# Four one-bank score accumulators in place of two two-bank tiles in branch B of an encoder layer

## The chip, the core and the metric

The kernel runs as one program on one core of a Trainium2 chip. The core has five engines with an instruction queue each: TensorE (PE in the profile, with its weight loads listed apart as PEld), VectorE (DVE), ScalarE (ACT), GpSimd (POOL) and SyncE (SP, which here only issues DMAs). Each engine takes its instructions in order; semaphores make one wait for another. Matmul results land in PSUM, eight banks of 512 float32 per partition. The metric is the device time of one execution in microseconds, lower is better. Before the change it is 2105.86 us, the median of three runs (2105.69 to 2107.47).

## The reference

One layer of an encoder with two token mixers runs over two sequences, `x_prompt` (1024 tokens) and `x_sample` (512 tokens), with a model width of 1024. The change sits in the second mixer, a neighbourhood attention on a grid 64 tokens wide:

```python
z = rmsnorm(x) @ w_in            # q_A k_A v_A q_B k_B v_B gate_A gate_B
o_a = grouped_query_attention(q_A, k_A, v_A)             # branch A
# branch B, 8 heads of 64, window of 8 rows x 16 columns:
s = einsum('bqhd,bkhd->bhqk', q_B, k_B) * scale + bias   # bias by 2-D offset
s = where(mask, s, -1e30)
o_b = softmax(s) @ v_B
mix = (sigmoid(gate_A) * (o_a @ w_proj_a) + sigmoid(gate_B) * (o_b @ w_proj_b)) @ w_out
x = x + mix
x = x + relu(rmsnorm(x) @ w_up)**2 @ w_down
y = rmsnorm(x)
```

## The kernel before

The two sequences are two trunks, s0 (512 tokens, names with `0_`) and s1 (1024 tokens, names with `1_`). Each goes through branch A, branch B (pool `phB0` or `phB1`) and a merge stage (`phG`); the MLP of both follows. Most matmuls are made of three (`mm3`, L266 to L268), from a high and a low part of each operand.

PSUM is shared out as two tiles of two banks (`pbig`, made by `big`, L90 and L108) and four tiles of one bank (`pmm`, made by `mm`). Branch A, the merge and others use both kinds.

Branch B works in units. A unit `u = (h, js)` is one head and, in s1, one of four column strips `j`, with two halves of the rows (`hf`); in s0 it is one head and a pair of strips, one half each. So a unit always has two score blocks, `x` = 0 and 1, called its halves below. `s_unit` computes them: for each half two matmuls into the scores (L1164, high and low part of the keys), one VectorE instruction that adds the bias and the mask and finds the row's extreme (L1166, which reads the scores in PSUM and writes `sbs`, with its accumulator into `msbs`), and the exponential on ScalarE (L1170). GpSimd makes the bias block (L1150). In s1 `planes` then normalises and splits the weights into two float16 planes (ScalarE L1191, VectorE L1192) and SP transposes them by DMA (L1195); in s0 `t_unit` transposes on PE (L1209). `v_unit` does the product with the values (L1237) and hands it on (L1244, L1245). Before the change both halves of a unit live in one `big` tile, each in its own bank:

```python
s = big(f"sb{N}_{h}_{js[0]}")
...
so = s[:, x * 512 : x * 512 + nkey]
for i in range(2):
    nc.tensor.matmul(so, q, kv[i], start=(i == 0), stop=(i == 1))
```

`nkey` is 384 in s1 and 256 in s0. Between the steps of a unit PE gets other work, pulled from a list (`fill`): the gate matmuls (`gps`), the projection of branch A (`ppas`, from L1040 on) and the projections of queries and keys (`pqb`, `pkb`).

The program's order is not written out by hand. The loop gives each engine its instructions, and the framework's scheduler then places them and works out the semaphores from the tiles and their buffers: a tile that takes over a buffer waits until the earlier one has been read. The order on each engine is fixed when the program is built.

Of the kernel before, what the change touches and what calls it, by code (L numbers as in the profile page):

```python
# [11 lines left out]
F32 = mybir.dt.float32  # L12
# [7 lines left out]
P = 128  # L20
# [54 lines left out]
def encoder(ctx: ExitStack, tc: tile.TileContext, xs, outs, w):  # L75
# [4 lines left out]
    mix = ctx.enter_context(ExitStack())  # L80
# [6 lines left out]
    rawp = mix.enter_context(tc.tile_pool(name="rawp", bufs=3))  # L87
    sgp = mix.enter_context(tc.tile_pool(name="sgp", bufs=2))
    s8l = mix.enter_context(tc.tile_pool(name="s8l", bufs=NLEFT))
    pbig = mix.enter_context(tc.tile_pool(name="pbig", bufs=2, space=bass.MemoryType.PSUM))  # L90
    pmm = mix.enter_context(tc.tile_pool(name="pmm", bufs=4, space=bass.MemoryType.PSUM))


    hd = dram.tile([NTOK, D], F32, name="hd")
# [2 lines left out]
    def phase(name, bufs=2):  # L97
        return tc.tile_pool(name=name, bufs=bufs, reuse_waits="tile")
# [8 lines left out]
        return pmm.tile([P, 512], F32, tag="mm", name=name)  # L107

    def big(name):
        return pbig.tile([P, 1024], F32, tag="big", name=name)  # L110


    ident = cst.tile([P, P], F32, name="ident")
# [28 lines left out]
    def first_norm(xt, gb, row, g8, ones, pool, nm):  # L142

        warm_up(6)
        pt = big("grow")
        for q in range(2):
            qs = slice(q * 512, q * 512 + 512)
            nc.tensor.matmul(pt[:, qs], ones, row[:, qs], start=True, stop=True)
        pg = mm("g8")[:, 0:NC8]
        tc.keep_in_program_order(nc.tensor.transpose(pg, g8, ident[0:NC8, 0:NC8]))  # L150
        gcol = sml.tile([P, 8], F32, tag="ms", name="gcol")
        xn = pool.tile([P, D], F32, tag="xn", name=f"xn{nm}", bufs=2)
        ss = sml.tile([P, 8], F32, tag="ss", name=f"ss{nm}")
        tc.keep_in_program_order(nc.scalar.activation(xn, xt, AF.Square, accum_out=ss[:, 0:1]))
        r = rstd(ss[:, 0:1], 1, D, nm, True)

        def spread():
            for q in range(2):
                qs = slice(q * 512, q * 512 + 512)
                tc.keep_in_program_order(nc.scalar.activation(gb[:, qs], pt[:, qs], AF.Copy))  # L160

        def rest():
            for q in range(2):
                qs = slice(q * 512, q * 512 + 512)
                tc.keep_in_program_order(
                    nc.vector.tensor_scalar(xn[:, qs], xt[:, qs], r[:, 0:1], None, op0=ALU.mult)
                )
            tc.keep_in_program_order(nc.vector.tensor_scalar(gcol, pg, 1.0, None, op0=ALU.mult))
            return xn, gcol

        return rest, spread, pt

    def warm_up(n):

        pt = big("warm")
        for i in range(n):
            nc.tensor.transpose(pt[:, i % 8 * P : (i % 8 + 1) * P], ident, ident)
# [172 lines left out]
    def transpose_tile(xn, dest, j, nm, pin=False, between=()):  # L350

        pt = big(f"pt{nm}")
        for c in range(NC8):
            nc.tensor.transpose(pt[:, c * P : (c + 1) * P], xn[:, c * P : (c + 1) * P], ident)
        view = [
            (
                pt[:, q * 512 : (q + 1) * 512].rearrange("p (c t) -> p c t", t=P),
                dest[0][q][:, :, j * P : (j + 1) * P],
                dest[1][q][:, :, j * P : (j + 1) * P],
            )  # L360
            for q in range(2)
        ]
        for src, hi, lo in view:
            op = nc.scalar.activation(hi, src, AF.Copy)
            if pin:
                tc.keep_in_program_order(op)
        for i, (src, hi, lo) in enumerate(view):
            for step in between[i : i + 1]:
                step()
            op = nc.vector.tensor_tensor(lo, src, hi.bitcast(F32), op=ALU.subtract)  # L370
            if pin:
                tc.keep_in_program_order(op)
# [120 lines left out]
    def run(tr, nxt, first):  # L493
        N, x, T, NT, NB = tr.N, tr.x, tr.T, tr.NT, tr.NB
# [83 lines left out]
        for g in range(2):  # L578
            with phase(f"phR{N}_{g}") as ph:
# [168 lines left out]
                for tt in range(NT):  # L748
                    tb, j = divmod(tt, 4)
                    nm = f"{N}_{g}_{tt}"  # L750
# [17 lines left out]
                    js = slice(j * P, (j + 1) * P)  # L768
# [115 lines left out]
            with phase(f"phA{N}_{g}") as ph:  # L884
# [79 lines left out]
                for ui, u in enumerate(units):  # L964
                    h, qb = u
# [88 lines left out]
        nkc = kr_n // 4  # L1054
        nkey = kr_n * 32
        nq = rows * 16
        with phase(f"phB{N}") as ph:
            JN = 3 - halves
            msk = ph.tile([P, halves * 3, nkey], BF16, tag="msk", name=f"msk{N}", bufs=1)
# [73 lines left out]

            def s_unit(u):
                h, js = u
                s = big(f"sb{N}_{h}_{js[0]}")
                p = ph.tile([P, 2, nkey], F32, tag="pb", name=f"pb{N}_{h}_{js[0]}", bufs=2)
                nm_, l, rl = (
                    sml.tile([P, 8], F32, tag=n_, name=f"{n_}b{N}_{h}_{js[0]}") for n_ in ("ms", "ss", "rs")
                )  # L1140
                for x, (j, hf) in enumerate((j, hf) for j in js for hf in range(halves)):
                    nm = f"{N}_{h}_{j}_{hf}"
                    ct = (0, 1, 1, 2)[j]
                    c0 = (0, 8, 24, 32)[j]
                    jr = (16, 8, 8, 0)[j]
                    r0 = 0 if hf == 0 else 4
                    ir = 4 if hf == 0 else 0
                    if j != 2:
                        bm = ph.tile([P, nkey], F32, tag="bm", name=f"bm{nm}", bufs=4)
                        nc.gpsimd.tensor_tensor(  # L1150
                            bm.rearrange("p (r c) -> p r c", c=32),
                            rects[h][:, ir : ir + kr_n, jr : jr + 32],
                            msk[:, hf * 3 + ct, :].rearrange("p (r c) -> p r c", c=32),
                            op=ALU.add,
                        )
                        bms[hf] = bm
                    bm = bms[hf]
                    q0 = j * (T // 4) + hf * P
                    so = s[:, x * 512 : x * 512 + nkey]
                    for i in range(2):  # L1160
                        kv = qk[h // 2][1][h % 2][:, i, :].rearrange("p (r c) -> p r c", c=GRID_W)[
                            :, r0 : r0 + kr_n, c0 : c0 + 32
                        ]
                        nc.tensor.matmul(so, qk[h // 2][0][:, h % 2, q0 : q0 + P], kv, start=(i == 0), stop=(i == 1))  # L1164
                    sb = ph.tile([P, nkey], F32, tag="sb", name=f"sbs{nm}", bufs=2)
                    nc.vector.tensor_tensor_reduce(  # L1166
                        out=sb, in0=so, in1=bm, op0=ALU.add, op1=ALU.min, scale=-1.0, scalar=3e38,
                        accum_out=nm_[:, x : x + 1],
                    )
                    nc.scalar.activation(  # L1170
                        p[:, x], sb, AF.Exp, bias=nm_[:, x : x + 1], scale=-1.0, accum_out=l[:, x : x + 1]
                    )
                    if JN == 2:
                        nc.vector.reciprocal(rl[:, x : x + 1], l[:, x : x + 1])
                        nc.gpsimd.tensor_scalar(p[:, x], p[:, x], rl[:, x : x + 1], 1.0, op0=ALU.mult, op1=ALU.mult)
                PT[u] = p
                if JN == 1:
                    rls[u] = l, rl
# [107 lines left out]
            n = len(units)  # L1286
# [4 lines left out]
            for i in range(n + LS + LV):  # L1291
                if NB == 1:
                    f = 9 if i < 1 else 5 if i < n - 4 else 6 if i < n else 4 if i == n else 2
                else:
                    f = 0 if i == n - 10 else 5 + (i % 3 > 0) if i < n - 8 else 7
                if JN == 1 and 0 < i <= n:
                    planes(units[i - 1])
                if i < n:
                    s_unit(units[i])
                    if units[i][1][0] == 1 and units[i][0] + 1 < 8:  # L1300
                        prep(units[i][0] + 1)
                    if i % per == (6 if JN == 1 else 2) and i + 2 < n:
                        while held:
                            held.pop(0)()
                        qp = qkproj(i // per + 1, wqk, qk)
                        for _ in range(NC8):
                            next(qp)
                    if i % per == per - 1 and qp is not None:
                        for _ in qp:
                            pass  # L1310
                        qp = None
# [19 lines left out]
            fill.drain()  # L1331


        mgs = {}
        with phase(f"phG{N}") as ph:
            oX = load_o(1) + oX3
# [35 lines left out]
            for c in range(NC8):  # L1372
# [4 lines left out]
                for tb in range(NB):  # L1377
# [4 lines left out]
                    nm = f"{N}_{c}_{tb}"  # L1382
# [33 lines left out]
            for half in range(2):  # L1416
                wo = wos[half]
                hc = slice(half * 512, half * 512 + 512)
                for tt in range(NT):
                    tb, j = divmod(tt, 4)  # L1420
                    nm = f"{N}_{half}_{tt}"
# [34 lines left out]
                    for k, i in todo:  # L1456
                        js = slice(i * P, (i + 1) * P)
# [603 lines left out]
    for i, tr in enumerate(trunks):  # L2061
        run(tr, trunks[i + 1] if i + 1 < len(trunks) else None, i == 0)
# [66 lines left out]
```

## Time and profile before

| | us |
|---|---|
| median of three runs | 2105.86 |
| the profiled execution | 2107.32 |
| its span, first to last instruction | 2105.5 |
| PE busy | 2071.3 (98%) |
| VectorE busy | 1500.9 (71%) |
| ScalarE busy | 1137.8 (54%) |
| GpSimd busy | 330.4 (16%) |
| mean granted clock of PE | 0.997 |

Branch B of s0 lies at about 178 to 300 us of the span, that of s1 at about 770 to 1025 us. In a row of the timeline stand the start, the time from the first to the last end, the engine, line and operation, the tile written and those read, the shape, a count where several of a kind follow each other, and in brackets the idle time of the engine just before with what ended it. Trailing numbers of tiles are left out there, so `sbs` stands for the score tiles of all units. Matmuls are pipelined: the next may start before the one ahead has ended.

### The profile page before, as it was taken

What the parts mean: (1) busy time and instruction counts of PE and PEld (TensorE: products, weight loads), DVE (VectorE), ACT (ScalarE), POOL (GpSimd) and SP (SyncE); (2) the same over time, 40 slices, a digit from 0 to 9 for tenths busy, and PEclk for the clock granted to TensorE, in tenths of its full rate; (3) what the DMA queues carried; (4) which work ended last, traced back from release to release, by engine and by line L of the source; (5) the groups of instructions that cost most, each with busy time, mean ns of one, the idle gap of its engine ahead of it and who ended that gap; (6) DMA issues with size and microseconds to landing.
All of it is one profiled execution on the core that took longest, in us unless ns stands there. A gap on an engine that the chain in (4) does not pass through costs nothing.

```text
span 2105.5 us, 31206 instructions
## 1 busy us (share of the span) xinstructions
PE 2071.3 (98%) x10521; PEld 1783.3 (85%) x10521; DVE 1500.9 (71%) x2885; ACT 1137.8 (54%) x2351; POOL 330.4 (16%) x445
## 2 busy tenths in 40 slices
PE   9999999999999999999999999999999999999998
PEld 8888878987797777777788999999999988888887
DVE  6775786778668855667864877787777777669563
ACT  5654654657647755666522666565556634334442
POOL 3232420422232222322101100012000000000000
PEclk9999999999999999999999999999999999999999
DMA  6546557645525565666764566478444899688561
GB/s 188 154 126 181 150 181 246 190 104 101 125 58 131 113 139 126 149 148 157 210 204 140 185 200 197 157 244 222 143 157 153 286 348 342 213 279 277 159 204 66
DMA packets 442569, 376.59 MB, mean 179 GB/s; under 512 B 167456, under 2 KB 380072, under 8 KB 442409
## 3 DMA queue, kind: packets, MB, share of 16 engines
q1 hardware_dynamic: 400471, 306.67, 50.4%
q10 hardware_dynamic: 36258, 50.88, 7.1%
q0 software_dynamic: 5680, 17.04, 2.9%
q8 instruction: 83, 1.36, 0.3%
q14 instruction: 77, 0.63, 0.1%
HBM read 263.29 MB, written 85.79 MB: 166 GB/s over the span
## 4 chain that ended last, share of the span: by engine, by line
PE 52%; DVE 1%; issue 1%; DMA 1%; ACT 1%; SPq 0%; POOL 0%; ACTq 0%; POOLq 0%; DVEq 0%
PE dn L267 7%; PE dn L268 7%; PE dn L266 7%; PE uc L266 2%; PE ud L266 2%; PE uc L268 2%; PE ud L268 2%; PE ud L267 2%; PE uc L267 2%; PE ua L266 2%; PE ua L268 2%; PE ua L267 2%; PE ops L267 1%; PE ops L268 1%; PE ops L266 1%; PE ub L266 1%
## 5 line engine op out<-in xcount | busy, mean ns | idle before, releaser
L268 PE MATMUL dn<-wd,al 128*128 128x512 f32 (+1 forms) x624 | 242.7, 389 | 0.0
L267 PE MATMUL dn<-wd,ah 128*128 128x512 f32 (+1 forms) x624 | 242.7, 389 | 0.0
L266 PE MATMUL dn<-wd,ah 128*128 128x512 f32 (+1 forms) x624 | 242.6, 389 | 0.0
L1542 ACT ACTIVATE ah<-ar 128x512 fp32r<-128x512 f32 x168 | 104.4, 627 | 202.5 <-PE dn L267 184.7
L1543 DVE TENSOR_TENSOR al<-ar,ah 128x512 fp32r<-128x512 f32 x168 | 115.0, 692 | 76.1 <-ACT ah L1542 68.1
L266 PEld LDWEIGHTS dn<-wd,ah 128*128 128x128 f32 x624 | 117.2, 188 | 24.2
L268 PEld LDWEIGHTS dn<-wd,al 128*128 128x128 f32 x624 | 117.2, 188 | 24.0
L267 PEld LDWEIGHTS dn<-wd,ah 128*128 128x128 f32 x624 | 117.2, 188 | 24.0
L903 ACT ACTIVATE ps<-ss,nms 128x1024 f32<-128x1024 f32 (+1 forms) x96 | 93.2, 971 | 33.9 <-DVE ls L911 11.9
L900 DVE TENSOR_REDUCE nms<-ss 128x1 f32<-128x1024 f32 (+1 forms) x96 | 99.7, 1039 | 13.9 <-PE ss L898 13.1
L266 PE MATMUL gpss<-xs_0h,w_gs 128*128 128x512 f32 x256 | 102.7, 401 | 1.4 <-DVE ptls L938 1.3
L267 PE MATMUL gpss<-xs_0l,w_gs 128*128 128x512 f32 x256 | 101.0, 395 | 0.0
L268 PE MATMUL gpss<-xs_0h,w_gs 128*128 128x512 f32 x256 | 100.7, 393 | 0.0
L251 POOL TENSOR_TENSOR rs_f<-ms_f,mhalf 128x1 f32<-128x1 f32 x6 | 4.0, 668 | 590.7 <-DVE ms_f L247 590.7
L1542 ACT ACTIVATE A<-S 128x512 fp32r<-128x512 f32 x128 | 76.1, 624 | 30.7 <-DVE S L1605 26.2
L1150 POOL TENSOR_TENSOR bms<-rects,msks 128x384 f32<-128x384 f32 (+1 forms) x72 | 64.2, 896 | 154.6 <-DVE msbs L1166 114.5
L1661 ACT ACTIVATE c<-c 128x384 f32<-128x384 f32 x97 | 50.7, 524 | 67.7 <-DVE c L1660 67.7
L1543 DVE TENSOR_TENSOR A<-S,A 128x512 fp32r<-128x512 f32 x128 | 84.5, 686 | 3.8 <-ACT A L1542 3.8
L1170 ACT ACTIVATE pbs<-sbss,msbs 128x384 f32<-128x384 f32 (+1 forms) x96 | 55.3, 577 | 58.8 <-POOL os_Bs L1263 23.3
L266 PE MATMUL uc<-B,A 128*128 128x384 f32 x256 | 85.7, 335 | 0.0
L266 PE MATMUL ud<-B,A 128*128 128x384 f32 x256 | 85.7, 335 | 0.0
L268 PE MATMUL uc<-B,A 128*128 128x384 f32 x256 | 85.7, 335 | 0.0
(391 smaller groups left out, 6369.2 us busy)
## 6 DMA issues: line engine op xcount, KB each, us to landing
ar<-ud SPq DMA_DIRECT2D x120, 512.0 KB
br<-in_w_mlp_down_dram SPq DMA_DIRECT2D x72, 512.0 KB
rawu<-in_w_mlp_up_dram SPq DMA_DIRECT2D x64, 512.0 KB
ud<-c ACTq DMA_DIRECT2D x128, 192.0 KB
raw_gs<-in_w_in_dram SPq DMA_DIRECT2D x32, 512.0 KB
zgs<-sgs ACTq DMA_DIRECT2D x48, 256.0 KB
ud<-cs SPq DMA_DIRECT2D x64, 192.0 KB
vss<-vds SPq DMA_DIRECT2D x256, 32.0 KB
```

Of the source, the lines that this page charges most:

```text
L251: nc.gpsimd.tensor_tensor(r[:, :n], m[:, :n], mhalf[:, :n], op=ALU.pow)
L266: nc.tensor.matmul(out, ah, bh, start=start, stop=False, **kw)
L267: nc.tensor.matmul(out, ah, bl, start=False, stop=False, **kw)
L268: nc.tensor.matmul(out, al, bh, start=False, stop=stop, **kw)
L900: nc.vector.tensor_reduce(nm_, s, axis=AX.X, op=ALU.max, negate=True)
L903: nc.scalar.activation(p, s, AF.Exp, bias=nm_, accum_out=l)
L1150: nc.gpsimd.tensor_tensor(bm.rearrange("p (r c) -> p r c", c=32), rects[h][:, ir : ir + kr_n, jr : jr + 32], msk[:, hf * 3 + ct, :].rearra ...
L1170: nc.scalar.activation(p[:, x], sb, AF.Exp, bias=nm_[:, x : x + 1], scale=-1.0, accum_out=l[:, x : x + 1])
L1542: nc.scalar.activation(hi, src, AF.Copy)
L1543: nc.vector.tensor_tensor(lo, src, hi.bitcast(F32), op=ALU.subtract)
L1661: nc.scalar.activation(t, t, AF.Relu)
```

## The change

Each half gets an accumulator of its own, one bank wide. For this the two-bank pool is closed at the start of branch B of each trunk and four one-bank buffers (`pbig1`, tag `one`) take its banks; before the merge stage the two-bank pool is opened again.

```diff
-    pbig = mix.enter_context(tc.tile_pool(name="pbig", bufs=2, space=bass.MemoryType.PSUM))
     pmm = mix.enter_context(tc.tile_pool(name="pmm", bufs=4, space=bass.MemoryType.PSUM))
+    bigs = mix.enter_context(ExitStack())
+    pbig = {}
+
+    def set_bigs(n):
+        bigs.close()
+        pbig.clear()
+        pbig[n] = bigs.enter_context(tc.tile_pool(name=f"pbig{n}", bufs=4 // n, space=bass.MemoryType.PSUM))
+
+    set_bigs(2)
...
     def big(name):
-        return pbig.tile([P, 1024], F32, tag="big", name=name)
+        return pbig[2].tile([P, 1024], F32, tag="big", name=name)
...
         nq = rows * 16
+        set_bigs(1)
         with phase(f"phB{N}") as ph:
...
             def s_unit(u):
                 h, js = u
-                s = big(f"sb{N}_{h}_{js[0]}")
...
-                    so = s[:, x * 512 : x * 512 + nkey]
+                    so = pbig[1].tile([P, 512], F32, tag="one", name=f"sb{nm}")[:, 0:nkey]
...
+        set_bigs(2)
         mgs = {}
         with phase(f"phG{N}") as ph:
```

Lines of the changed kernel stand 8 or 9 further down: L1164 becomes L1172, L1166 becomes L1174, L1192 becomes L1200, L1237 becomes L1245, and `mm3` is at L274 to L276. The number of instructions of each kind stays the same; their order on the engines and their waits change inside the two branches B. Two places on PE follow. A name like `sbs1_2_3` is the score tile of s1, head 2, strip 3; after the change `sbs1_2_3_0` and `sbs1_2_3_1` are its two halves. The last number of a name is only a counter.

PE in s1 at unit 2_3 (the place of the stall at 856 us in the trace), before the change:

```order
L1237 MATMUL obs1_2_1_9774<-bhs1_2_1_9663,vss1_2_9197 128x2x128
L1164 MATMUL sbs1_2_3_9796<-kBs1_1_0_9340,qBs1_1_9339 128x384 x2
L266 MATMUL gpss1_3328_3_1_9752<-xs1_1h1_4693,w_gs1_3328_3_9290 128x512
...
L266 MATMUL gpss1_3328_4_0_9827<-xs1_0h0_4286,w_gs1_3328_4_9639 128x512
L1164 MATMUL sbs1_2_3_9796<-kBs1_1_0_9340,qBs1_1_9339 128x384 [waits DVE_49]
L1164 MATMUL sbs1_2_3_9796<-kBs1_1_0_9340,qBs1_1_9339 128x384
L267 MATMUL gpss1_3328_4_0_9827<-xs1_0l0_4288,w_gs1_3328_4_9639 128x512
```

and after it:

```order
L1245 MATMUL obs1_2_1_9813<-bhs1_2_1_9700,vss1_2_9230 128x2x128
L1172 MATMUL sbs1_2_3_0_9841<-kBs1_1_0_9375,qBs1_1_9374 128x384 x2
L1172 MATMUL sbs1_2_3_1_9849<-kBs1_1_0_9375,qBs1_1_9374 128x384 [waits DVE_49]
L1172 MATMUL sbs1_2_3_1_9849<-kBs1_1_0_9375,qBs1_1_9374 128x384
L274 MATMUL gpss1_3328_3_1_9791<-xs1_1h1_4717,w_gs1_3328_3_9324 128x512
L275 MATMUL gpss1_3328_3_1_9791<-xs1_1l1_4719,w_gs1_3328_3_9324 128x512
```

The second half's two matmuls moved up past 13 gate matmuls, to right behind the first half's. The wait on VectorE that they carry is now for their buffer, which an earlier unit's half held.

PE in s1 near 974 us, where scores of several units stand together (`ppas` is the projection of branch A), before:

```order
L268 MATMUL ppas1_0_1_11044<-oXs1_0_3_10913,w_pas1_0_10889 128x512
L1164 MATMUL sbs1_6_0_11100<-kBs1_3_0_10699,qBs1_3_10698 128x384 x2
L1164 MATMUL sbs1_6_3_11178<-kBs1_3_0_10699,qBs1_3_10698 128x384 [waits DVE_49]
L1164 MATMUL sbs1_6_3_11178<-kBs1_3_0_10699,qBs1_3_10698 128x384
L1164 MATMUL sbs1_6_0_11100<-kBs1_3_0_10699,qBs1_3_10698 128x384 [waits DVE_49]
L1164 MATMUL sbs1_6_0_11100<-kBs1_3_0_10699,qBs1_3_10698 128x384
L1164 MATMUL sbs1_7_1_11255<-kBs1_3_1_10700,qBs1_3_10698 128x384 [waits DVE_49,Activation_49]
L1164 MATMUL sbs1_7_1_11255<-kBs1_3_1_10700,qBs1_3_10698 128x384
L1164 MATMUL sbs1_6_3_11178<-kBs1_3_0_10699,qBs1_3_10698 128x384 [waits DVE_49]
L1164 MATMUL sbs1_6_3_11178<-kBs1_3_0_10699,qBs1_3_10698 128x384
L266 MATMUL ppas1_1_0_11066<-oXs1_0_0_10895,w_pas1_1_10985 128x512 [waits PE_49,Activation_49]
```

and after (each half's second matmul follows its first; those of the middle halves are left out):

```order
L1172 MATMUL sbs1_6_0_0_11160<-kBs1_3_0_10750,qBs1_3_10749 128x384 [waits DVE_49]
...
L1172 MATMUL sbs1_6_0_1_11168<-kBs1_3_0_10750,qBs1_3_10749 128x384 [waits DVE_49]
...
L1172 MATMUL sbs1_6_3_0_11239<-kBs1_3_0_10750,qBs1_3_10749 128x384 [waits DVE_49]
...
L1172 MATMUL sbs1_6_3_1_11247<-kBs1_3_0_10750,qBs1_3_10749 128x384 [waits DVE_49]
...
L1172 MATMUL sbs1_7_1_0_11317<-kBs1_3_1_10751,qBs1_3_10749 128x384 [waits DVE_49]
...
L1172 MATMUL sbs1_7_1_1_11325<-kBs1_3_1_10751,qBs1_3_10749 128x384 [waits DVE_49]
...
L1172 MATMUL sbs1_7_2_0_11384<-kBs1_3_1_10751,qBs1_3_10749 128x384 [waits DVE_49]
L1172 MATMUL sbs1_7_2_0_11384<-kBs1_3_1_10751,qBs1_3_10749 128x384
L274 MATMUL ppas1_1_0_11120<-oXs1_0_0_10947,w_pas1_1_11038 128x512 [waits PE_49,Activation_49]
```

Four more matmuls moved into this row, the second half of unit 7_1 and the first of 7_2 (whose second half stays about a hundred rows further down). VectorE's reads of these scores follow in the same sequence, with the planes of units 6_1 and 6_2 (L1200, `hbs`) between them:

```order
L1200 SCALAR_TENSOR_TENSOR hbs1_6_1_0_11073<-pbs1_6_1_10994,rsbs1_6_1_10997,hbs1_6_1_0_11073 128x3x128 [waits DMAHW2_49,Activation_49]
L1174 ISA sbss1_6_0_0_11163,msbs1_6_0_11155<-sbs1_6_0_0_11160,bms1_6_0_0_11158 128x384 [waits PE_49]
...
L1200 SCALAR_TENSOR_TENSOR hbs1_6_1_1_11077<-pbs1_6_1_10994,rsbs1_6_1_10997,hbs1_6_1_1_11077 128x3x128 [waits DMAHW3_49,Activation_49]
L1200 SCALAR_TENSOR_TENSOR hbs1_6_2_0_11146<-pbs1_6_2_11081,rsbs1_6_2_11084,hbs1_6_2_0_11146 128x3x128 [waits DMAHW4_49,Activation_49]
L1174 ISA sbss1_6_0_1_11171,msbs1_6_0_11155<-sbs1_6_0_1_11168,bms1_6_0_1_11166 128x384 [waits PE_49]
...
L1174 ISA sbss1_6_3_0_11242,msbs1_6_3_11234<-sbs1_6_3_0_11239,bms1_6_3_0_11237 128x384 [waits PE_49,Activation_49,Pool_49]
```

Here the plane of unit 6_2 (`hbs1_6_2_0`) stands ahead of the read of 6_0's second half; before, it came behind 6_3's first read.

## The prediction

> **What bounds the kernel now.** I read the page first: part 1 for the engines, part 2 for the clock.
>
> ```profile
> span 2105.5 us, 31206 instructions
> PE 2071.3 (98%) x10521; PEld 1783.3 (85%) x10521; DVE 1500.9 (71%) x2885; ACT 1137.8 (54%) x2351; POOL 330.4 (16%) x445
> ```
>
> PE is the bound: 2105.5 - 2071.3 leaves 34.2 us in which it had no matmul. No other engine is above 71%. An edit that adds or removes no instruction can win only what PE loses by waiting, by restarting, or by running at a low clock. So the next view is the windows, one row for each stage (columns: stretch, its length, busy time of PE, PEld, DVE, ACT, POOL with instruction counts, granted clock, DMA share, GB/s).
>
> ```profile
> 178.00:270.00 92.00, 91.28 (x448) 73.45 (x447) 58.11 (x150) 52.09 (x106) 36.12 (x51) 1.00 0.54 160
> 270.00:300.00 30.00, 28.72 (x150) 23.25 (x149) 25.41 (x73) 20.49 (x45) 9.07 (x15) 1.00 0.52 153
> ...
> 780.00:1025.00 245.00, 232.42 (x1034) 177.91 (x1035) 169.51 (x410) 148.45 (x292) 65.12 (x71) 0.99 0.66 151
> 1025.00:1200.00 175.00, 174.89 (x838) 149.55 (x837) 114.31 (x189) 63.88 (x110) 20.44 (x27) 1.00 0.57 187
> 1200.00:1700.00 500.00, 500.00 (x2823) 489.68 (x2822) 377.51 (x630) 302.32 (x596) 24.52 (x29) 1.00 0.63 200
> ```
>
> Branch B of the second trunk (s1, about 770 to 1025 us) loses 245.00 - 232.42 = 12.6 us, over a third of all PE idle time; branch B of the first (s0, 178 to 300 us) loses 2.0 us; from 1025 to 1700 us PE is full. The waits of PE name the cause (us in total, times, longest):
>
> ```profile
> PE sbs L1164 <- DVE msbs L1166: 13.5, 18, 3.8
> PE pTs L933 <- POOL pns L923: 2.4, 5, 1.1
> PE os L954 <- DMA PTs<-hls: 1.9, 5, 0.7
> ```
>
> 13.5 us in 18 stalls are score matmuls (L1164) that wait for VectorE's reduction over an earlier score (L1166). The next waits belong to branch A, which the change leaves alone. One stall, row by row on PE:
>
> ```profile
> 854.16 0.39 PE L268 MATMUL gpss<-xs_0h,w_gs 128*128 128x512 f32 x1
> 854.39 0.39 PE L266 MATMUL gpss<-xs_0h,w_gs 128*128 128x512 f32 x1
> 856.27 0.62 PE L1164 MATMUL sbs<-kBs,qBs 128*128 128x384 f32 x2 [1.49 <-DVE msbs L1166]
> 856.72 0.39 PE L267 MATMUL gpss<-xs_0l,w_gs 128*128 128x512 f32 x1
> ```
>
> A gate matmul is 0.39 us long, but its successor starts 0.23 us after it: matmuls overlap by 0.16 us. From the last gate matmul to the score matmul pass 856.27 - 854.39 = 1.88 us instead of 0.23, so a stall shown as 1.49 us costs 1.65: the idle time and the lost overlap.
>
> **The change, part by part.** No instruction is added or removed; buffers and order change. Before, the second half's matmuls carry a wait on VectorE's read of the first half, although they write the other bank of the tile. The order of after has the four matmuls of a unit in a row in most places, and the wait that a half then carries is for its buffer, read four halves (two units) ago.
>
> *Term 1, the stalls: 13.5 us*, the row above. *Term 2, the lost overlap:* 18 x 0.16 = 2.9 us.
>
> *Term 3, the second visit.* The group's row (ns: least, median, longest), then a pair that did not wait, and a run of four:
>
> ```profile
> L1164 PE MATMUL sbs<-kBs,qBs x192: 279/343/561, 181.2 to 1020.3; 128*128 128x384 f32 x128, 128*128 128x256 f32 x64
> ...
> 972.05 0.61 PE L1164 MATMUL sbs<-kBs,qBs 128*128 128x384 f32 x2
> 972.50 0.40 PE L267 MATMUL ppas<-oXs,w_pas 128*128 128x512 f32 x1
> ...
> 974.33 0.87 PE L1164 MATMUL sbs<-kBs,qBs 128*128 128x384 f32 x4
> 976.72 0.62 PE L1164 MATMUL sbs<-kBs,qBs 128*128 128x384 f32 x2 [1.52 <-DVE msbs L1166]
> 978.21 1.52 PE L1164 MATMUL sbs<-kBs,qBs 128*128 128x384 f32 x4 [0.86 <-DVE msbs L1166]
> 979.53 0.64 PE L266 MATMUL ppas<-oXs,w_pas 128*128 128x512 f32 x1
> 979.97 0.63 PE L267 MATMUL ppas<-oXs,w_pas 128*128 128x512 f32 x1
> ```
>
> A pair between long matmuls takes 972.50 - 972.05 = 0.45 us from start to start. In the run of four, three steps and one matmul of 0.343 us take 0.87: 0.175 a step, 0.35 a pair. Two visits pay the 0.10 us twice, a run of four once: 192 matmuls are 48 units (16 in s0, 32 in s1), and 48 x 0.10 = 4.8 us. Bounds: 0, if a run pays it at its end as two pairs did, and 4.8; I take 4.8, since the run in the row shows the short step.
>
> *Term 4, the clock.* After the longest stall PE went on slowly:
>
> ```profile
> 1001.08 0.40 PE L266 MATMUL ppas<-oXs,w_pas 128*128 128x512 f32 x1
> 1005.25 0.73 PE L1164 MATMUL sbs<-kBs,qBs 128*128 128x384 f32 x2 [3.77 <-DVE msbs L1166]
> 1005.77 0.63 PE L267 MATMUL ppas<-oXs,w_pas 128*128 128x512 f32 x1
> ...
> 1008.75 0.53 PE L268 MATMUL ppas<-oXs,w_pas 128*128 128x512 f32 x1
> 974.00:984.00 10.00, 7.62 (x29) 5.37 (x28) 9.42 (x25) 6.45 (x16) 5.29 (x6) 0.83 0.68 162
> 1004.00:1009.00 5.00, 3.75 (x10) 3.11 (x11) 4.70 (x11) 1.85 (x7) 2.47 (x3) 0.66 0.54 120
> ```
>
> Seven steps take 1008.75 - 1005.77 = 2.98 us, 0.43 each instead of 0.23: 1.4 us lost, and the windows (the last two rows) show a granted clock of 0.66 there, and 0.83 around the three stalls at 974 to 980, where 979.97 - 979.53 = 0.44 is a slow step too. About five such steps make 1.0 us. Term 4 is 2.4 us at most. [...]
>
> The four terms: 13.5 + 2.9 + 4.8 + 2.4 = 23.6 us. Now what is late next.
>
> *The cluster at 974 us.* Before, ten score matmuls stood in a row there, with two stalls inside. In after it is fourteen, for halves of units 6_0, 6_3, 7_1 and 7_2; with four buffers, the fifth half waits for the read of the first, the sixth for the second, the seventh for the third. VectorE there, before:
>
> ```profile
> 974.00 2.19 DVE L1192 SCALAR_TENSOR_TENSOR hbs<-pbs,rsbs,hbs 128x384 f16<-128x384 f32 x2
> 976.12 0.54 DVE L1166 CUSTOM_DVE_ANT_0 sbss<-sbs,bms 128x384 f32<-128x384 f32 x1
> ...
> 977.98 0.55 DVE L1166 CUSTOM_DVE_ANT_0 sbss<-sbs,bms 128x384 f32<-128x384 f32 x1
> 978.46 0.08 DVE L1166 DVE_READ_ACCUMULATOR2_ANT msbs<- 128x1 f32 x1
> ```
>
> The third read (unit 6_3, first half) ended at 978.5 and stays behind the same planes work in after. Unstalled, the fourteen would end at 974.33 + 14 x 0.175 = 976.8; held to about 979, they lose 2.2 us, and 0.3 for restarts: 2.5 us stay. So may the slow second at 979: 1.0 us stays.
>
> *First halves.* Their wait for a buffer was hidden; only one of them shows a stall (0.86 us, the x4 row at 978.21). Standing earlier, after four matmuls instead of two, they may meet it elsewhere. Bounds: 0, and term 1 again (13.5 us, every stall replaced by one like it). I take 2.6 us, a fifth of term 1, near the lower end, because 31 of 32 first halves of s1 are unstalled now.
>
> *The pools.* The bank pool is closed and opened at the start and the end of branch B. The work before it used these banks in branch A, and no row of the order there gains a wait that is not VectorE's or ScalarE's usual one. Cost 0; if it waited once per switch as the longest wait in branch A (POOL pns, 1.1 us), four switches would cost 4.4 us.
>
> *The queues.* On SP one bias load (rects) moves ahead of two transposes in s1, and a few weight pieces move behind transposes. The gate and projection matmuls do not wait for weights now, except 0.7 us once:
>
> ```profile
> PE ppas L266 <- ACT sgs L528: 0.7, 1, 0.7
> ```
>
> Cost 0, bound 4.2 us, six late pieces of that size.
>
> Sum: 23.6 - 2.5 - 1.0 - 2.6 = **17.5 us**. The profiled execution took 2107.32 us (1.8 us beside its span), so 2089.8 from it; it is 1.46 us above the median of the runs, 2105.86, from which I forecast 2105.86 - 17.5 = **2088.4 us**. Of the 17.5 about 2 to 3 us fall into s0.
>
> **Rivals.**
>
> *A, the wait moves on.* A unit's chain goes scores, VectorE, ScalarE's exponential, planes, transposes, then the value matmuls (L1237). PE meets the value matmuls a fixed number of rows later; without stalls it comes sooner and might wait there, or VectorE paces the stage. Against it: value matmuls show no idle time at all, and VectorE itself waits for PE's scores.
>
> ```profile
> L1237 PE MATMUL obs<-bhs,vss 128*128 128x512 f16 (+1 forms) x192 | 37.4, 315 | 0.0
> L1166 DVE CUSTOM_DVE_ANT_0 sbss<-sbs,bms 128x384 f32<-128x384 f32 (+1 forms) x96 | 48.4, 506 | 27.9 <-PE sbs L1164 25.1 <-issue 1.3 <-POOL pbs L1175 0.7
> ```
>
> VectorE is busy 169.51 of 245 us there, so on average it has slack, but at 974 to 984 it is busy 9.42 of 10. If terms 1 and 2 come back whole, terms 3 and 4 remain: up to 7.2, less 2.6, so about 4.6 us: 2101.3. Chance 0.15.
>
> *B, slower: reads behind planes.* A second half's matmuls now stand where the first half's do, and PE takes them in order. Where VectorE has put a pair of planes (2.19 us, the row at 974.00) ahead of the read that frees their buffer, PE stands 2.19 us with all gate work queued behind. At 23.6 us to win, this decides from 11 units (24.1 us); in one unit of three, 16, it costs 35.0, and the time is 2105.86 + 11.4 = 2117.3. For it: the cluster. Against: the buffer is two units old, and the reads follow their scores soon where VectorE isn't full. Chance 0.05.
>
> *C, no effect.* The waits could be tied to something else than the tile. Against: in the order the second half's wait disappears or goes to the buffer. Then 2105.9. Chance 0.04.
>
> *D, a long leftover.* If the cluster's three waits merge into one of 3.8 us, as at 1005, it loses 4.0 us and the 1.4 us of slow steps instead of 2.5 and 1.0, that is 1.9 us more: 2090.3. Its mark is a clock under 0.8 in those 5 us. [...] Chance 0.06.
>
> [...]
>
> **How the numbers follow.** Forecast 0.70, A 0.15, D 0.06, B 0.05, C 0.04. The forecast's own range is 2081 to 2097: at the lower end all of 23.6 us and a little, at the upper 13.5 + 2.9 less 2.5, 1.0 and half of the queues' and pools' bounds. The range of 8 in 10 adds D and most of A: 2080 to 2103. Left out are B, C, the last of A (0.05) and tails of the forecast. What a measurement of this kernel can tell from no change is about 0.2%, 4.2 us, so faster means under 2101.6 and slower over 2110.1. Faster: 0.70 + 0.06 + half of A = 0.84; same: the other half of A and C, 0.11; slower: B, 0.05.
>
> **What would show it.** In the profile after, the row of PE waiting at the score matmuls for VectorE should fall from 13.5 to 3 to 6 us, most of it near 970 us; PE's busy time in s1's branch B stays within 3 us while the stage gets 13 to 18 us shorter; the clock at the former 1004 to 1009 us is 1.00. Term 3 is right if a run of four and its successor take 0.8 us from start to start rather than 0.9. The forecast is wrong if PE's idle time under L1237 or at the projection's matmuls rises by more than 5 us (A), or if the stalls at the score matmuls stay above 10 us (B, C).

## The result, and the profile after

| | before | after |
|---|---|---|
| median of four runs, us | 2106.34 | 2092.42 |
| lowest to highest, us | 2105.69 to 2107.47 | 2090.49 to 2092.83 |
| ratio of the runs | | 0.9932, 95% interval 0.9914 to 0.9949 |
| span of the profiled execution, us | 2105.5 | 2090.9 |

The change saves 13.9 us by the medians, 14.6 us by the spans. In two experiments below an execution was disturbed (7112 us of the kernel before, 5311 us of the run with an own value bank); neither enters a median or a ratio here, and the second one's profile is not read.

The page of the changed kernel, its span and part 1:

```profile
span 2090.9 us, 31196 instructions
PE 2063.8 (99%) x10521; PEld 1783.2 (85%) x10521; DVE 1497.1 (72%) x2885; ACT 1138.0 (54%) x2351; POOL 331.4 (16%) x445
```

Without a matmul were 2090.9 - 2063.8 = 27.1 us, 7.1 less than before. That is only half of the 14.6, because busy time holds part of what is lost: before the change PE counted as busy for all 3.41 us from 1005.62 to 1009.03 us, at a granted clock of 0.50, and the stall shown as 1.49 us at 856 us cost 1.65 us from start to start. So the stages are read from their lengths, from the first score matmul of a branch to its last value matmul:

| us | before | after | difference |
|---|---|---|---|
| up to branch B of s0 | 181.2 | 181.1 | -0.1 |
| branch B of s0 | 122.7 | 122.1 | -0.6 |
| from there to branch B of s1 | 466.2 | 463.6 | -2.6 |
| branch B of s1 | 263.3 | 251.0 | -12.3 |
| the rest | 1072.1 | 1073.1 | +1.0 |

The waits of PE after the change (us in total, times, longest):

```profile
PE obs L1245 <- DMA bhs<-hbs: 2.7, 3, 1.3
PE sbs L1172 <- DVE msbs L1174: 2.5, 2, 1.6
PE pTs L941 <- POOL pns L931: 1.6, 5, 0.4
...
PE sbs L1172 <- DVE kBs L1136: 1.1, 2, 0.6
...
PE ptbs L1217 <- POOL pbs L1183: 0.6, 2, 0.4
PE ppas L274 <- ACT w_pas L263: 0.6, 1, 0.6
```

Score matmuls that wait for VectorE's reads went from 13.5 us in 18 stalls to 2.5 in 2. At the top stands a wait that was not there: value matmuls that wait for the transposes. The start of branch B of s1 shows it, and next to it the form that a unit now has (timeline of PE):

```profile
779.30 0.39 PE L276 MATMUL gpss<-xs_0h,w_gs 128*128 128x512 f32 x1
781.02 0.81 PE L1245 MATMUL obs<-bhs,vss 128*128 128x512 f16 x4 [1.33 <-DMA bhs<-hbs]
781.59 0.96 PE L1172 MATMUL sbs<-kBs,qBs 128*128 128x384 f32 x4
782.39 0.40 PE L274 MATMUL gpss<-xs_0h,w_gs 128*128 128x512 f32 x1
```

Four score matmuls and the step to the next take 782.39 - 781.59 = 0.80 us. Before them PE stood 1.33 us. Before the change the value matmuls of this unit started at 783.98 us and met no wait; score matmuls had stalled for 0.79 us at 780.31 ahead of them. Counted from the branch's first score matmul, they start after 14.2 us now and started after 14.0 us before: what PE saved up to here it waits for the transposes.

The one place where score matmuls still stall is the bunch of fourteen:

```profile
961.76 1.58 PE L1172 MATMUL sbs<-kBs,qBs 128*128 128x384 f32 x8
964.25 0.63 PE L1172 MATMUL sbs<-kBs,qBs 128*128 128x384 f32 x2 [0.91 <-DVE msbs L1174]
966.49 1.25 PE L1172 MATMUL sbs<-kBs,qBs 128*128 128x384 f32 x4 [1.61 <-DVE msbs L1174]
967.75 0.80 PE L274 MATMUL ppas<-oXs,w_pas 128*128 128x512 f32 x1
968.35 0.63 PE L275 MATMUL ppas<-oXs,w_pas 128*128 128x512 f32 x1
```

and the window there (columns as in the windows of before):

```profile
965.00:975.00 10.00, 8.50 (x31) 5.91 (x32) 8.81 (x23) 6.57 (x15) 3.97 (x5) 0.83 0.96 225
```

Eight matmuls (four halves) run through, the fifth half waits 0.91 us for its buffer, the sixth 1.61, together 2.5 us. The window shows the clock at 0.83, as it was at 974 to 984 us before the change. The long stall at 1005 us of before (3.77 us) is gone with its slow steps.

VectorE's row shows the other side: its waits for score matmuls fell from 25.1 to 9.9 us.

```profile
L1174 DVE CUSTOM_DVE_ANT_0 sbss<-sbs,bms 128x384 f32<-128x384 f32 (+1 forms) x96 | 47.0, 503 | 14.2 <-PE sbs L1172 9.9 <-POOL pbs L1183 1.7 <-issue 1.4
```

### The profile page after: what moved, and what is told of

It reads as the page before. It is cut to its first block, busy times and chain, and to the rows that moved or that the text cites. A ratio compares the mean times of both kernels' runs of the same rounds, so it can differ in the third digit from the quotient of the medians.

```text
span 2090.9 us, 31196 instructions
## 1 busy us (share of the span) xinstructions
PE 2063.8 (99%) x10521; PEld 1783.2 (85%) x10521; DVE 1497.1 (72%) x2885; ACT 1138.0 (54%) x2351; POOL 331.4 (16%) x445
## 4 chain that ended last, share of the span: by engine, by line
PE 65%; DVE 5%; DMA 3%; issue 3%; ACT 2%; POOL 1%; ACTq 0%; SPq 0%; POOLq 0%; DVEq 0%
PE dn L276 7%; PE dn L275 7%; PE dn L274 7%; PE uc L274 2%; PE ud L276 2%; PE uc L276 2%; PE ud L274 2%; PE ud L275 2%; PE uc L275 2%; PE ua L276 2%; PE ua L274 2%; PE ua L275 2%; PE gpss L276 2%; PE gpss L275 2%; PE gpss L274 2%
## 5 line engine op out<-in xcount | busy, mean ns | idle before, releaser
L276 PE MATMUL dn<-wd,al 128*128 128x512 f32 (+1 forms) x624 | 242.3, 388 | 0.0
L274 PE MATMUL dn<-wd,ah 128*128 128x512 f32 (+1 forms) x624 | 242.3, 388 | 0.0
L274 PEld LDWEIGHTS dn<-wd,ah 128*128 128x128 f32 x624 | 117.1, 188 | 24.2
L276 PEld LDWEIGHTS dn<-wd,al 128*128 128x128 f32 x624 | 117.1, 188 | 24.1
L274 PE MATMUL gpss<-xs_0h,w_gs 128*128 128x512 f32 x256 | 102.5, 400 | 1.4 <-DVE ptls L946 1.3
L276 PE MATMUL gpss<-xs_0h,w_gs 128*128 128x512 f32 x256 | 100.6, 393 | 0.0
L274 PE MATMUL uc<-B,A 128*128 128x384 f32 x256 | 85.6, 334 | 0.2 <-ACT s L1686 0.2
L274 PE MATMUL ud<-B,A 128*128 128x384 f32 x256 | 85.6, 334 | 0.0
L276 PE MATMUL ud<-B,A 128*128 128x384 f32 x256 | 85.5, 334 | 0.0
L275 PE MATMUL ud<-B,A 128*128 128x384 f32 x256 | 85.5, 334 | 0.0
```

Of the source, the lines that this page charges most:

```text
L274: nc.tensor.matmul(out, ah, bh, start=start, stop=False, **kw)
L275: nc.tensor.matmul(out, ah, bl, start=False, stop=False, **kw)
L276: nc.tensor.matmul(out, al, bh, start=False, stop=stop, **kw)
```

## The experiments

Two questions are open after this. Where do the gain and the part given back lie (theory: s1's score stalls bring it, and new waits for transposes and banks take some back)? And what in the change does it: the four separate buffers, or just that the second half is not ordered behind the first half's read?

**One trunk at a time.** `e1_s1_only` keeps the two-bank tile in s0, `e2_s0_only` keeps it in s1 (the same with `halves == 1`):

```diff
-        set_bigs(1)
+        if halves == 2:
+            set_bigs(1)
...
             def s_unit(u):
                 h, js = u
+                s = None if 1 in pbig else big(f"sb{N}_{h}_{js[0]}")
...
-                    so = pbig[1].tile([P, 512], F32, tag="one", name=f"sb{nm}")[:, 0:nkey]
+                    so = (
+                        s[:, x * 512 : x * 512 + nkey] if s is not None
+                        else pbig[1].tile([P, 512], F32, tag="one", name=f"sb{nm}")[:, 0:nkey]
+                    )
...
-        set_bigs(2)
+        if 1 in pbig:
+            set_bigs(2)
         mgs = {}
```

> One-bank accumulators in the branch B of s1 alone; s0 keeps the halves of a two-bank tile. If the gain is that of s1's score stalls: branch B of s1 about 251 us long as after (263.3 before), branch B of s0 back at 122.7 us with its score stalls, time 2092 to 2094. Rival (the two trunks share the gain in the ratio of their 18 and 4 us of lost score time, so s0 gave 2 us or more): 2095 or more.

> One-bank accumulators in the branch B of s0 alone. If s0's stalls only moved to the transposes, value matmuls and projection: branch B of s0 0.3 to 0.8 us shorter, time 2104.5 to 2106.5, and the stretch from there to the branch B of s1 (466.2 us before, 463.6 after) back at 465 to 466.5, so that its 2.6 us were scatter between executions. Rival (s0's change also shortens that stretch): 463.6 there and a time near 2103.

`e1_s1_only`: 2092.52 us (ratio 0.9933, 0.9919 to 0.9947), the time of the whole change; branch B of s1 248.9 us, of s0 122.4. `e2_s0_only`: 2106.15 us (0.9998, 0.9989 to 1.0007), no effect; branch B of s0 121.7 us, the stretch after it 464.5. That stretch was 466.2, 463.6, 465.4 and 464.5 us in four executions of before, after and these two, with no sign of following the edit by itself. Taken together with branch B of s1 it is steadier: 729.5 us before and 729.4 in `e2_s0_only`, 714.6 after and 714.3 in `e1_s1_only`. So the change in s1 is worth about 15 us over both; how that divides between them (12.3 and 2.6 us in the table) is not settled by one trace of each kernel. The waits of the two, `e1_s1_only` first:

```profile
PE sbs L1177 <- DVE msbs L1179: 3.5, 6, 1.6
```

```profile
PE sbs L1177 <- DVE msbs L1179: 13.5, 14, 4.6
```

Nearly all the stall time belongs to s1. In s0 PE stalled 0.8 us at scores, 0.7 us for a sigmoid and 0.2 us at a transpose before; with the change it stalls 2.7 us in seven places, none of them VectorE's reads of scores: weights, transposes' inputs, keys, queries, that sigmoid.

**Order or buffers.** `e4_two_bank_ahead` is the kernel before with its two two-bank tiles; only the text of `s_unit` changes, so that both halves' matmuls come ahead of both reads:

```diff
+                sos = []
                 for x, (j, hf) in enumerate((j, hf) for j in js for hf in range(halves)):
...
                         nc.tensor.matmul(so, qk[h // 2][0][:, h % 2, q0 : q0 + P], kv, start=(i == 0), stop=(i == 1))
+                    sos.append((nm, x, so, bm))
+                for nm, x, so, bm in sos:
                     sb = ph.tile([P, nkey], F32, tag="sb", name=f"sbs{nm}", bufs=2)
```

> The kernel before with its two two-bank tiles, but in the program the four score matmuls of a unit are written ahead of VectorE's two reads, so that the second half's matmuls carry no wait on the first half's read. If the stall comes from the order of write and read inside one tile, not from the banks: score stalls fall to 2 to 5 us as after, time 2091 to 2095. Rival (the gain needs four accumulators that are freed one by one): the stalls come back as waits for the buffer, 8 us or more, and the time is 2098 or more.

2098.22 us (2097.13 to 2098.42; ratio 0.9958, 0.9945 to 0.9971). The stalls are what the first expectation said, the time is in the rival's range: neither holds whole. It takes 8.6 of the 14 us. PE's waits:

```profile
PE sbs L1165 <- DVE msbs L1169: 3.6, 1, 3.6
PE os L954 <- DMA PTs<-hls: 2.5, 6, 0.6
PE ppas L266 <- ACT w_pas L255: 2.2, 1, 2.2
```

The eighteen stalls are one. So the stalls come from the order of write and read within one tile, which needs no other banks to be undone. What is missing to the change, nearly 6 us, is only in part accounted for: branch B of s1 takes 254.0 us instead of 251.0 (one longer stall in the bunch, 2.2 us for a late weight after it), and the stretch before it takes 467.6 us, the longest of all runs. That is not a mark of two-bank tiles, for a run with one-bank tiles below has 467.0 there; its cause stays open. So the order explains the stalls, and what separate buffers add to it was not isolated.

`e7_three_buffers` gives the changed kernel three one-bank buffers:

```diff
-        pbig[n] = bigs.enter_context(tc.tile_pool(name=f"pbig{n}", bufs=4 // n, space=bass.MemoryType.PSUM))
+        pbig[n] = bigs.enter_context(tc.tile_pool(name=f"pbig{n}", bufs=2 if n == 2 else 3, space=bass.MemoryType.PSUM))
```

> The changed kernel with three one-bank accumulators instead of four, so that a half waits for the half three earlier. If what counts is that a half no longer waits for its neighbour's read: outside the bunch the reads are long done, score stalls 3 to 6 us, time 2092.5 to 2096. Rival (two whole units must be in flight): stalls of 8 us or more, time 2099 or more.

2093.64 us (2091.70 to 2094.61; ratio 0.9941, 0.9926 to 0.9956), as expected of the theory: the intervals of three and four buffers overlap. PE's waits:

```profile
PE sbs L1172 <- DVE msbs L1174: 2.9, 2, 1.6
PE obs L1245 <- DMA bhs<-hbs: 2.2, 3, 0.9
```

The fourth buffer makes no difference that can be measured here, and the waits given back are of the same kind.

**The wait given back.** `e3_lv2` is the changed kernel with the value matmuls of s1 one unit later:

```diff
-            LS, LV = 1, 1
+            LS, LV = 1, (2 if JN == 1 else 1)
```

> The changed kernel with the value matmuls of s1 one unit later (lag of 3 units instead of 2). If the transposes are what PE now meets too early: the waits of PE at the value matmuls for transposes (2.7 us in three stalls) lose those at the start of the branch, 1.6 us, and the time falls by 1 to 3 us, to 2089.5 to 2091.5. Rival (the chain through VectorE and ScalarE paces the start of the branch, so that PE waits at the next scores instead): same time as after within 0.7 us.

2092.67 us (0.9935, 0.9921 to 0.9949), no gain. The waits for transposes went, all of them, and another came:

```profile
PE pqbs L274 <- DVE os_Bs L1253: 3.1, 3, 1.5
PE sbs L1172 <- DVE msbs L1174: 2.6, 2, 1.7
```

The query projection `pqb` now waits for a bank of the four-bank pool that holds the value matmuls' result until VectorE has read it (`os_B`). So 2.7 us became 3.1. Branch B of s1 is 1.7 us shorter even so (249.3 us), but the stretch before it is 1.4 us longer, and the merge stage has a wait that the changed kernel does not have there:

```profile
PE ppbs L274 <- ACT oXs L1283: 1.4, 1, 1.4
```

The rival was right about the time, though the place is a bank, not the scores.

`e10_own_value_bank` therefore gives that result the bank that three score buffers leave free, with the same lag; `e11_both` adds the earlier weight of `e9_second_weight_early` below.

```diff
-                o = mm(f"ob{nm}")
+                o = pbig[1].tile([P, 512], F32, tag="ob", name=f"ob{nm}", bufs=1)
```

> Three one-bank score accumulators, the fourth bank given to the value matmuls' result, and the value matmuls of s1 one unit later. With the lag alone PE waited 3.2 us for a bank that VectorE had still to empty. If that was what took the lag's gain: no waits at the value matmuls for transposes nor at the query projection for that bank (under 1 us together), branch B of s1 247 to 249 us, time 2089 to 2091. Rival (VectorE paces the branch whatever bank is free): 2092 to 2094, the waits under other names.

> Both of the two before: own bank and later value matmuls, and the second weight piece early. If the two are separate leftovers, the gains add: 2085.5 to 2088.5. Rival (each only moves the wait): 2091 or more.

2095.44 us (0.9948, 0.9935 to 0.9962) and 2097.39 us (0.9961, 0.9947 to 0.9974). The first is slower than either side expected, though its interval overlaps that of the change; the second is in its rival's range (2091 or more), with every execution above the slowest of the change. Waits of `e11_both`:

```profile
PE obs L1248 <- DVE os_Bs L1256: 4.3, 6, 1.3
PE ppas L274 <- ACT w_pas L263: 2.3, 2, 1.6
```

One bank is too few: a unit's value matmuls wait until VectorE has read the unit ahead. The wait went to the third place. The edit gives s0 the single bank too, so part of the loss lies there: 1.1 us of such waits (the row below), and its branch B takes 123.8 us instead of 122.1.

```profile
PE obs L1248 <- DVE os_Bs L1261: 1.1, 2, 0.7
```

**The bunch.** It stands where the projection of branch A (`ppa`) begins and its second weight piece, issued on SP at 960.6 us in the changed kernel, reaches PE at 967.75. Two ways to make it early, `e5_early_weights` (the whole projection's loads two units earlier; `e6_before_early_weights` and `e8_two_bank_early` are the same on the kernel before and on `e4_two_bank_ahead`):

```diff
-                if i == n - (6 if first else 9):
+                if i == n - (6 if first else 11):
                     pa = proj_a(ph, held)
```

> The changed kernel, with the loads for the projection of branch A started two units earlier in s1 (n - 11 instead of n - 9). The fourteen score matmuls at 962 us then stand apart again, with projection matmuls between them. If the leftover of 2.5 us and the slow steps after it come from that bunch: both go, branch B of s1 is 3 to 4 us shorter than with the change alone (250.95), time 2088 to 2090. Rival (the next projection weight is late anyway and PE waits for it instead): 2092 to 2093.

> The kernel before with the same earlier loads. Its bunch at 974 us goes (1.52 and 0.86 us of stall, about 1 us of slow steps), and perhaps the stall of 3.77 us at 1005, where VectorE was busy with late weights; the stalls of the second halves elsewhere stay: 6 to 10 us of score stalls, time 2098 to 2104. Rival (the scheduler's bunch is independent of them): 2106.

> Two two-bank tiles with the four score matmuls written ahead of the reads, and the earlier loads. If what two-bank tiles lacked (2098.2 against 2092.5) lies in the bunch, where a unit waits for both reads of an earlier one: the stall of 3.55 us and the 2.2 us for late weights go, and the time is that of the changed kernel with earlier loads, within 1.5 us. Rival (the first read waits for all four matmuls and the whole branch suffers): 4 us or more above it.

`e5_early_weights`: 2098.28 us (0.9966, 0.9954 to 0.9979), slower than the change by 6 us, which neither side expected. No score stall for VectorE's reads is left in s1, but:

```profile
PE pqbs L274 <- ACT sgs L536: 3.8, 1, 3.8
PE obs L1245 <- DMA bhs<-hbs: 3.7, 2, 2.4
```

The first is again a bank: the gate's sum is freed by ScalarE's sigmoid (`sgs`). On ScalarE the splits of what is now loaded early stand ahead of it (timeline of ScalarE):

```profile
939.49 0.62 ACT L1199 ACTIVATE hbs<-pbs,rsbs 128x384 f16<-128x384 f32 x1 [3.26 <-DMA obds<-os_Bs]
940.01 0.62 ACT L263 ACTIVATE w_pas<-raw_pas 128x512 fp32r<-128x512 f32 x1
940.53 1.99 ACT L263 ACTIVATE oXs<-rawos 128x1024 fp32r<-128x1024 f32 x2
...
945.24 0.63 ACT L263 ACTIVATE w_pas<-raw_pas 128x512 fp32r<-128x512 f32 x1 [0.18 <-DMA raw_pas<-in_w_proj_a_dram]
945.78 0.58 ACT L536 ACTIVATE sgs<-gpss 128x512 f32<-128x512 f32 x1
```

In the 9.5 us before the sigmoid, 3.26 are a wait and 3.2 are these splits; which of the two made it late was not tried. After the stall of 3.8 us, which ends at 946.4, the clock is low again: 0.52 from 945 to 952 us.

```profile
945.00:952.00 7.00, 5.59 (x13) 4.43 (x14) 5.79 (x18) 5.33 (x12) 2.52 (x3) 0.52 0.45 140
```

`e6_before_early_weights`: 2101.87 us (0.9981, 0.9972 to 0.9990), 4 us faster than before, as expected: its waits show 10.5 us in 17 stalls with a longest of 2.6, so the stalls of the second halves stay when the bunch is taken apart (6 to 10 us of stalls were expected).

```profile
PE sbs L1164 <- DVE msbs L1166: 10.5, 17, 2.6
```

`e8_two_bank_early`: 2097.31 us (0.9966, 0.9954 to 0.9979), within 1 us of `e5_early_weights` as the first side expected, but this tells little: both carry the new sigmoid stall (2.8 us here), and against `e4_two_bank_ahead` (2098.22) the intervals tell no gain.

The narrower way, `e9_second_weight_early`, loads only the second piece ahead; `e12_two_weights_early` also the third:

```diff
             oA = load_o(0, hold)
+            w_1 = None if first else load_cols(w["w_proj_a"][0], P, P, f"pa{N}_1", slot_left)
             yield
             for c in range(NC8):
                 wp = nxt_w
-                if c + 1 < NC8:
+                if c == 0 and w_1 is not None:
+                    nxt_w = w_1
+                elif c + 1 < NC8:
```

> The changed kernel with only the second weight piece of the projection of branch A (pa1_1) loaded ahead, right behind the loads that stand there already; nothing else starts earlier. If the bunch exists because that weight is late: the leftover score stalls (2.5 us) and the slow steps (about 1 us) go without the 3.8 us stall of the run that started everything two units earlier; branch B of s1 247 to 248.5 us, time 2088.5 to 2090.5. Rival (any earlier load on SP delays the transposes behind it, and PE waits at the value matmuls by as much): 2092 or more.

> As the run with the second weight piece early, and the third piece (pa1_2) ahead too, before the transposes of unit 5_3 on SP. There PE's largest wait near 970 us was for that third piece (1.83 and 0.49 us). If it is only its load that is late: those 2.3 us go, branch B of s1 246 to 247 us, time 2088 to 2090. Rival (the fourth piece is late in its place, or the transposes of unit 5_3, now behind the load, hold up the value matmuls): 2090.5 to 2093.

`e9_second_weight_early`: 2090.93 us (2090.12 to 2094.75), ratio 0.9931 (0.9919 to 0.9944), the ratio of the change itself; the time lies between the two sides. Branch B of s1 is 248.0 us long as expected, but the stretch before it is 467.0 us, so that both together are no shorter than with the change (715.0 and 714.6 us). The bunch and its 2.5 us are gone, and there are waits for the next weight: 1.83 us for its high part (the row below has 0.6 us of s0 in it) and 0.49 us for its low part.

```profile
PE ppas L274 <- ACT w_pas L263: 2.5, 2, 1.8
...
PE obs L1248 <- DMA bhs<-hbs: 1.8, 2, 1.0
```

`e12_two_weights_early`: 2093.63 us (0.9948, 0.9935 to 0.9962), just above the rival's range, and branch B of s1 takes 250.3 us. The weights are on time, and PE waits at the value matmuls, not for transposes as the rival had it, but mostly for a bank that VectorE has still to read:

```profile
PE obs L1248 <- DVE os_Bs L1256: 4.7, 4, 1.9
...
PE ppas L274 <- DVE os_Bs L1256: 1.6, 2, 1.3
```

No version was clearly faster than the change.

## Why the prediction came out as it did

The forecast was 2088.4 us, the range 2080 to 2103, and faster with a chance of 0.84; it came out at 2092.4, faster. Mechanism and place were right: the second half's matmuls stand behind the first half's, their stalls are gone, and s1 carries the gain. Of the forecast 17.5 us, 13.9 came. That it came so near is in part luck: an allowance of 2.6 us that was not needed covered nearly half of the 6 us that the sum had at nothing. By steps:

- *Terms 1 to 4.* Sum the start-to-start times of PE in both branches B beyond the usual step (0.227 us after a matmul of 512 columns, 0.173 for 384, 0.120 for 256): score matmuls lost 24.8 us before (4.1 in s0, 20.7 in s1) and lose 6.1 after (1.0 and 5.1). That is 18.7 us won at the place itself, where the forecast had 17.5 after its deductions.
- *Term 3* was mis-sized. Four in a row take 0.80 us to the next step, as it said, but summed over all units the second visit's excess fell by about 3 us (second matmuls of the halves: 7.6 to 4.6), not 4.8.
- *The deductions.* The bunch: 2.5 us forecast, 0.91 + 1.61 = 2.5 measured, and the slow steps stayed. They were put too low: the clock is 0.50 from 967.27 to 970.68 us, which at half speed loses about 1.7 us (an estimate from these two numbers) where the forecast had 1.0; term 4 had each of its two slow stretches too low in the same way (978.31 to 981.73 and 1005.62 to 1009.03 us before the change, both at 0.50). The allowance of 2.6 us for first halves was too much: outside the bunch no half waits for VectorE's read of its buffer in s1. That buffers are hardly needed, `e7_three_buffers` shows: three do it.
- *Rival A, which I kept out of the sum, came in part,* and this is the step that failed. I took the value matmuls' zero idle time as the sign that nothing was near, and cost the queues at 0. Here that zero showed no slack: the value matmuls came late themselves, and once PE reaches the first of s1 sooner, it waits there 1.33 us. By the same sum as above, value matmuls lose 4.7 us now (0.6 before), transposes on PE in s0 1.9 (0.5), a few projections 1 us more and the gates 0.8 us less: about 6 us of the 18.7 given back. What remains in the two branches is 12.9 us. The stretch between them (2.6 us shorter) and the rest (1.0 longer) make it 14.6 by the spans.
- *s0* was to give 2 to 3 us. It gave 0.6, and `e2_s0_only` no difference that can be measured: here rival A holds nearly whole: 3.1 us won at the scores, about 2.7 given back at transposes, value matmuls and projections.
- *Rivals B, C and D* did not come. The waits at the bunch are two, 0.91 and 1.61 us with a matmul pair between them. The mark set for D, a clock under 0.8 in those 5 us, did come (0.66 from 966 to 971 us), so it does not tell one long wait from two shorter ones.
- *What would show it:* the row of score waits was to fall to 3 to 6 us and fell to 2.5; the stage was to get 13 to 18 us shorter and got 12.3; the former place of the 3.77 us stall was to be at clock 1.00, and is (990 to 1012 us). PE's busy time in branch B of s1 was to stay within 3 us and fell by 6.0 (250.4 to 244.4): that mark did not fit the forecast's own terms 2 to 4, since part of what they win back had counted as busy (a slow step filled 0.43 us, a usual one 0.23). The mark set for A, over 5 us at the value matmuls or the projections, was not reached by the waits alone (3.1 us at the value matmuls, 2.7 of them for transposes), though nearly by all that is lost there.

That the given-back part is a chain of near-limits, not one wait, was tried from four sides: take away the transposes' wait and a bank is late (`e3_lv2`), give that bank and it is late itself (`e11_both`), take away the bunch and the next weight is late (`e9_second_weight_early`), and bring that early and VectorE's `os_B` is late (`e12_two_weights_early`). In each, the new wait is 2 to 5 us. That these waits are one chain is argued from the four results; what would take away all of them together was not found.

## What to carry to other kernels

In this kernel two results shared a tile, and the framework ordered the second's writes behind the first's read, although they went to another bank; splitting the tile took the stalls from 13.5 us to 2.5. Just writing both matmuls ahead of both reads left one stall of 3.6 us and brought only 8.6 of the 14 us. The row of the waits (13.5 us) came near the gain (13.9), but only because lost overlap, second visits and clock on one side and new waits on the other nearly cancel. Then look at what the stalled engine meets next: the value matmuls, downstream of the stalls, showed an idle time of zero before and waits of 3.1 us after, and of 18.7 us won at the place about 6 came back as small waits for transposes, banks and weights. Loads brought forward put 3.2 us of splits ahead of a sigmoid on ScalarE (`e5_early_weights`), and PE waited 3.8 us for the bank that this sigmoid frees; how much of that the splits made was not tried.

## What the runs showed of the hardware

After some stalls PE went on slowly, after others at once. In the changed kernel it idled 0.91 and 1.61 us with 0.63 us of work between; the granted clock was 0.50 from 967.27 to 970.68 us, and steps took 0.43 us instead of 0.23. In `e9_second_weight_early` it idled 1.83 and 0.49 us; steps of 0.43 us followed (973.05 to 973.48), and the clock was 0.90 in the window. In `e4_two_bank_ahead` a single stall of 3.55 us was followed by a step of 0.43 us (971.78 to 972.21). A single stall of 1.49 us before the change was followed by steps of 0.23 us at once, and one of 2.36 us in `e5_early_weights` by steps of 0.32 and 0.23 us (from 1022.80). What decides between the two was not shown.

The rows are a window of the changed kernel, then PE's timeline and a window of `e9_second_weight_early`, then the timelines of `e4_two_bank_ahead` and `e5_early_weights`:

```profile
967.27:970.68 3.41, 3.40 (x9) 2.03 (x8) 3.06 (x7) 2.10 (x5) 1.04 (x2) 0.50 0.83 207
```

```profile
971.23 0.50 PE L274 MATMUL ppas<-oXs,w_pas 128*128 128x512 f32 x1 [1.83 <-ACT w_pas L263]
971.57 0.40 PE L275 MATMUL ppas<-oXs,w_pas 128*128 128x512 f32 x1
972.45 0.50 PE L276 MATMUL ppas<-oXs,w_pas 128*128 128x512 f32 x1 [0.49 <-DVE w_pas L269]
972.79 0.46 PE L274 MATMUL ppas<-oXs,w_pas 128*128 128x512 f32 x1
973.05 0.63 PE L275 MATMUL ppas<-oXs,w_pas 128*128 128x512 f32 x1
973.48 0.63 PE L276 MATMUL ppas<-oXs,w_pas 128*128 128x512 f32 x1
965.00:975.00 10.00, 7.68 (x32) 5.04 (x30) 6.36 (x18) 4.67 (x12) 2.80 (x3) 0.90 0.84 205
```

```profile
970.37 1.62 PE L1165 MATMUL sbs<-kBs,qBs 128*128 128x384 f32 x4 [3.55 <-DVE msbs L1169]
971.78 0.63 PE L266 MATMUL ppas<-oXs,w_pas 128*128 128x512 f32 x1
972.21 0.63 PE L267 MATMUL ppas<-oXs,w_pas 128*128 128x512 f32 x1
```

```profile
1022.24 0.81 PE L1245 MATMUL obs<-bhs,vss 128*128 128x512 f16 x4 [2.36 <-DMA bhs<-hbs]
1022.80 0.48 PE L274 MATMUL ppbs<-oXs,w_pbs 128*128 128x512 f32 x1
1023.12 0.40 PE L275 MATMUL ppbs<-oXs,w_pbs 128*128 128x512 f32 x1
1023.35 0.40 PE L276 MATMUL ppbs<-oXs,w_pbs 128*128 128x512 f32 x1
```
